# Root-mean-square norms of a transformer kernel: squares, sums and row scale issued at three separate places

## The chip, the cores and the metric

The kernel runs on one core of a Trainium2 chip. Its time is the device time in microseconds (us) of one execution; lower is better. The engines are named as in the profile: PE does the matrix products and PEld loads their stationary operands, DVE is the vector engine, ACT the activation engine, POOL the general one (GpSimd), SP issues the transfers.

## The reference

256 tokens of 1024 features go through two blocks of attention and feed-forward parts, a mixture of experts among them. Every part begins with the same norm, and this norm is what the change is about:

```python
def rms_norm(x, g):
    xf = x.astype(F32)
    y = xf * lax.rsqrt(jnp.mean(xf * xf, axis=-1, keepdims=True) + EPS)
    return (y * g.astype(F32)).astype(x.dtype)
...
    h = rms_norm(x, a_norm_mix[j])
    x = x + diff_attention_mixer(h, mem, ...)
    ...
    x = x + dense_swiglu(rms_norm(x, dense_norm[j]), dense_w_gate_up[j], dense_w_down[j])
```

The gain g is folded into the operand of the products. The factor 1/rms is one number per token and commutes with a product over the features, so the kernel multiplies the unscaled x and scales what comes out.

## The kernel before

The activations x lie with the features on the partitions: four tiles of 128 x 512 (`xpair(i)`, two blocks of 128 features by 256 tokens). Each weight piece of 128 x 1024 is split into a high and a low part, `hi` by ACT (L229) and `lo` by DVE (L230); x is split in the same way into `xh` and `xl`. A product is then three matmuls, xh with hi, xh with lo and xl with hi (L258 to L260 by features, L264 to L266 by tokens). PE does almost nothing else, and it works strictly in the order of its instructions, as do DVE, ACT and POOL. A list scheduler of the framework sets that order when the kernel is built, from the order of the code and its own costs; each instruction waits only for its data and its buffers.

A norm (`stats_r`, 16 of them) goes as follows. ACT squares the four tiles (L334). In the eleven norms of the kind "later", POOL adds them in pairs (L337), so that two tiles of 128 x 512 are left. PE sums over the features: it multiplies each 128 x 128 piece of those tiles with one column of ones (L350, tile `ms`), eight matmuls of 128 x 1, each of which stands in the trace as two records. DVE adds epsilon (L353), POOL takes the power -1/2 (L354): that is `r`, by token on the partitions. Products by features need it along the free dimension: `rows_R` turns it on PE with two transposes (L361, tile `R`), and DVE copies the result out (L365). The eleven are those of layer A, of the memory `mem`, of the dense part, of layer B, of the mixture of experts, and of the start, the feed-forward part and the gate at the end ("ple") of each of the two last blocks. The five others (`final_norm` and the four norms after a part, in `post`) add their squares on DVE (L339) and stand where nothing else is left to multiply.

In the code before, sums and turn stand right behind the squares: `R = stats_R(xpair)`. The scheduler places the first four thin matmuls as soon as it takes the first pair to be ready, the other four when the second pair is, and the transposes a few products behind.

Of the kernel before, what the change touches and what calls it, by code (L numbers as in the profile page):

```python
# [17 lines left out]
EPS = 1e-6  # L18
# [76 lines left out]
# vectors over the features, as columns of 128: (key, how many columns)  # L95
# [15 lines left out]
def layout(v):  # L111
    """the arrays of the launch: the weights as they come, the rest laid out as the chip reads it"""
# [21 lines left out]
def body(ctx: ExitStack, tc: tile.TileContext, I, out, stop=None):  # L134
# [111 lines left out]
    def wpieces(w, k0, kn, c0, width, s):  # L246
        """wtile in pieces of 512, which leaves its tiles to what is under way"""
# [120 lines left out]
    def stats_R(src):  # L368
        return rows_R(stats_r(src))

    def stats(src):
        r = stats_r(src)
        return r, rows_R(r)

# [32 lines left out]
    def feat_1024(X, w, s, order, side=None, hook=None):  # L407
        """X times w, by features; side yields what it makes of X while the rest is multiplied"""
# [67 lines left out]
    def steps(gen, n=None):  # L476
        """runs n steps of a generator (all of them without n); whether it goes on"""
# [10 lines left out]
    def feat_gen(X, w, c0, s, done, loaded=None):  # L488
        wh, wl = wsplit(loaded or wload(w, 0, 8, c0, 256, s))
        ps = PB("fp")  # L490
        for k in range(8):
# [3 lines left out]
            if k == 3:  # L495
                yield 1
        done(ps)
        yield 1

    def tok_gen(X, w, c0, s, done):  # L500
        wh, wl = wtile(w, 0, 8, c0, 256, s)
        ps = PB("tp")
        for k in range(8):
# [3 lines left out]
            if k == 3:  # L507
                yield 1
        done(ps)
        yield 1  # L510

    def feat_pair(X, w, c0, s):
        out = []
        steps(feat_gen(X, w, c0, s, out.append))
        return out[0]
# [4 lines left out]
    def by_R(lst, R, f=None, tile=G):  # L520
        """keeps a product by features, times R"""
        def done(ps):
            g = tile("fT")
            if f is None:
                V.tensor_tensor(r3(g, 2), r3(ps, 2), R2(R), op=OP.mult)
            else:
                V.scalar_tensor_tensor(r3(g, 2), r3(ps, 2), f, R2(R), op0=OP.mult, op1=OP.mult)
# [1310 lines left out]
```

## Time and profile before

| what | value |
|---|---|
| median of 3 runs | 2311.73 us (2307.82 to 2312.98) |
| span of the profiled execution | 2313.2 us |
| instructions | 36939 |
| PE busy | 2239.2 us, 97% of the span |
| DVE busy | 1817.8 us, 79% |
| ACT busy | 1474.7 us, 64% |
| POOL busy | 76.4 us, 3% |
| the thin matmuls of all 16 norms (L350) | 256 records, 35.0 us busy |

The profiled execution is one of its own; its span is 0.06% above the median of the timed runs. Busy times of PE overlap from one matmul to the next, so a busy PE can still be slowed: the granted clock (PEclk) says how fast it could go, 1.00 at the higher of its two levels (2.4 GHz) and 0.50 at the lower (1.2 GHz).

### The profile page before, as it was taken

Reading aid. Unit: us, or ns where it says so; the run is one execution under the profiler, and the core shown is the slowest. Engines: PE = TensorE matmul, PEld = TensorE weight load, DVE = VectorE, ACT = ScalarE, POOL = GpSimd, SP = SyncE. Lnnn points to the kernel's source line nnn. Section 1 sums busy time; section 2 is a strip of 40 time slices with the busy share of each in tenths; the row PEclk is TensorE's granted clock in tenths of the full one; section 3 lists DMA queues with packets and bytes.
Section 4 is the critical chain, followed back from the end, with each engine's and each line's share of the span. In section 5 each row is a group of like instructions: output and inputs, shape, how many; then the busy total and the mean of one; then the engine's idle time right before and its main releaser. Section 6 shows DMA issues by size and latency. Waiting matters only on the chain. (4 is left out here: it accounts for less than half of the span.)

```text
span 2313.2 us, 36939 instructions
## 1 busy us (share of the span) xinstructions
PE 2239.2 (97%) x14218; PEld 2019.2 (87%) x14218; DVE 1817.8 (79%) x2701; ACT 1474.7 (64%) x2138; POOL 76.4 (3%) x83
## 2 busy tenths in 40 slices
PE   8999999998999999999999999999999999989998
PEld 7889999997878888888888888879899998989998
DVE  6666576766888898989898989888777777867776
ACT  5554457435777777777777777777665565765554
POOL 0100001000000000000000000000000001000001
PEclk9999999998999999999999999999999999989998
DMA  8445556224999999999999999986245544525550
GB/s 288 139 137 174 195 171 204 92 78 167 359 348 335 349 353 372 338 354 351 373 350 341 349 378 350 372 299 221 74 136 193 182 147 137 186 78 183 183 178 19
DMA packets 297113, 551.23 MB, mean 238 GB/s; under 512 B 10336, under 2 KB 132064, under 8 KB 296928
## 3 DMA queue, kind: packets, MB, share of 16 engines
q1 hardware_dynamic: 296928, 548.78, 67.5%
q8 instruction: 114, 1.87, 0.3%
q14 instruction: 71, 0.58, 0.1%
HBM read 547.70 MB, written 1.05 MB: 237 GB/s over the span
## 5 line engine op out<-in xcount | busy, mean ns | idle before, releaser
L230 DVE TENSOR_TENSOR loe<-ste,hie 128x1024 fp32r<-128x1024 f32 x448 | 520.0, 1217 | 12.4 <-ACT hie L229 4.2
L229 ACT ACTIVATE hie<-ste 128x1024 fp32r<-128x1024 f32 x448 | 439.5, 1053 | 23.9 <-PE ac L260 9.9
L230 DVE TENSOR_TENSOR lod<-std,hid 128x1024 fp32r<-128x1024 f32 x224 | 264.9, 1218 | 17.1 <-ACT hid L229 15.6
L229 ACT ACTIVATE hid<-std 128x1024 fp32r<-128x1024 f32 x224 | 221.4, 1057 | 4.8 <-PE pg L265 2.3
L266 PE MATMUL pu<-loe,eh 128*128 128x512 f32 x448 | 176.7, 394 | 1.4 <-DVE loe L230 1.4
L1159 PE MATMUL y<-hid,hl 128*128 128x512 f32 x448 | 175.7, 392 | 2.0 <-DVE hl L284 2.0
L264 PE MATMUL pg<-hie,eh 128*128 128x512 f32 x448 | 175.4, 391 | 0.3 <-ACT eh L286 0.3
L266 PE MATMUL pg<-loe,eh 128*128 128x512 f32 x448 | 175.6, 392 | 0.0
L264 PE MATMUL pu<-hie,eh 128*128 128x512 f32 x448 | 174.7, 390 | 0.0
L265 PE MATMUL pg<-hie,el 128*128 128x512 f32 x448 | 174.6, 390 | 0.0
L265 PE MATMUL pu<-hie,el 128*128 128x512 f32 x448 | 174.6, 390 | 0.0
L1158 PE MATMUL y<-hid,hh 128*128 128x512 f32 x448 | 173.4, 392 | 0.7 <-ACT hh L283 0.7
L1137 ACT ACTIVATE eh<-pg,cw 128x512 f32<-128x512 f32 x56 | 38.6, 689 | 203.4 <-PE pg L266 203.4
L1160 PE MATMUL y<-lod,hh 128*128 128x512 f32 x448 | 163.4, 407 | 0.8
L258 PE MATMUL gu<-xh,hig 128*128 128x256 f32 x528 | 150.8, 286 | 3.7 <-ACT xh L286 3.7
L230 DVE TENSOR_TENSOR lou<-stu,hiu 128x1024 fp32r<-128x1024 f32 x66 | 80.4, 1220 | 91.1 <-PE gu L259 82.9
L259 PE MATMUL gu<-xh,log 128*128 128x256 f32 x528 | 150.5, 285 | 0.0
L260 PE MATMUL gu<-xl,hiu 128*128 128x256 f32 x528 | 150.5, 285 | 0.0
L258 PE MATMUL gu<-xh,hiu 128*128 128x256 f32 x528 | 150.4, 285 | 0.0
L259 PE MATMUL gu<-xh,lou 128*128 128x256 f32 x528 | 150.3, 285 | 0.0
L260 PE MATMUL gu<-xl,hig 128*128 128x256 f32 x528 | 150.1, 285 | 0.0
L258 PE MATMUL ac<-hh,hidn 128*128 128x256 f32 x528 | 149.4, 283 | 0.0
(516 smaller groups left out, 6279.5 us busy)
## 6 DMA issues: line engine op xcount, KB each, us to landing
ste<-in_moe_w_gate_up_dram SPq DMA_DIRECT2D x224, 1024.0 KB, 7.2
std<-in_moe_w_down_dram SPq DMA_DIRECT2D x112, 1024.0 KB, 5.5
stg<-in_w_up_dram SPq DMA_DIRECT2D x22, 1024.0 KB, 5.1
stu<-in_w_up_dram SPq DMA_DIRECT2D x22, 1024.0 KB, 5.1
stdn<-in_w_down_dram SPq DMA_DIRECT2D x22, 1024.0 KB, 4.8
stg<-in_dense_w_gate_up_dram SPq DMA_DIRECT2D x11, 1024.0 KB, 5.0
stu<-in_dense_w_gate_up_dram SPq DMA_DIRECT2D x11, 1024.0 KB, 5.0
stdn<-in_dense_w_down_dram SPq DMA_DIRECT2D x11, 1024.0 KB, 4.9
```

The lines of the kernel that those rows point to most:

```text
L229: A.activation(hi[:, :m], sq, AF.Copy)
L230: V.tensor_tensor(lo[:, :m], sq, hi.bitcast(F32)[:, :m], op=OP.subtract)
L258: T.matmul(o, lhsT=lh, rhs=rh, start=start, stop=False, **kw)
L259: T.matmul(o, lhsT=ll, rhs=rh, start=False, stop=False, **kw)
L260: T.matmul(o, lhsT=lh, rhs=rl, start=False, stop=stop, **kw)
L264: T.matmul(o, lhsT=xh, rhs=wh, start=start, stop=False, **kw)
L265: T.matmul(o, lhsT=xl, rhs=wh, start=False, stop=False, **kw)
L266: T.matmul(o, lhsT=xh, rhs=wl, start=False, stop=stop, **kw)
L1137: A.activation(t, pg, AF.Silu, scale=rc)
L1158: T.matmul(y[hf], lhsT=h[:, fs], rhs=a, start=opens, stop=False)
L1159: T.matmul(y[hf], lhsT=l[:, fs], rhs=a, start=False, stop=False)
L1160: T.matmul(y[hf], lhsT=h[:, fs], rhs=b, start=False, stop=ends)
```

## The change

The eleven norms become objects of a class `Norm` with three parts. The squares are made at once; POOL adds only the first two tiles, DVE adds the third and the fourth (L368 of the changed kernel, 128 x 512) and then the halves (L369, 128 x 256), so that 256 columns are left and two thin matmuls do where eight did (four records for sixteen). These are issued when something first asks for `r`, and the transposes when something first asks for `R`. `first_two` asks for r behind the first whole product and for R in the middle of the second; `swiglu_ff` asks for r at step 20 of the 32 of its first pair and for R when that pair is done; `tok_wide` at its second half; the memory's norm does its squares early and its sums at the end of the second group of filling work. The five others (`stats_now`) keep their eight thin matmuls, with the last square made in two halves.

```diff
-    def squares(src, how):
-        """tiles whose sum over features, through the matrix of ones, is the mean square"""
-        sq = [J("sq") for _ in range(4)]
-        for i in range(4):
-            A.activation(sq[i], src(i), AF.Square)
-            if how == "later":
-                if i % 2:
-                    GP.tensor_tensor(sq[i - 1], sq[i - 1], sq[i], op=OP.add)
-            elif i in (1, 2):
-                V.tensor_tensor(sq[0], sq[0], sq[i], op=OP.add)
-        return sq[0:3:2] if how == "later" else sq[0:4:3]
-
-    def stats_r(src, how="later"):
-        """1 / rms over the 1024 features, by token"""
-        tiles = squares(src, how)
+    def mean_square(pieces):
         ps = PC("ms")
-        for n, t in enumerate(tiles):
+        for n, t in enumerate(pieces):
             for c in range(2):
-                for kk in range(2):
-                    o = kk * 256 + c * 128
-                    T.matmul(ps[:, c:c + 1], lhsT=t[:, o:o + 128], rhs=onec, start=n == 0 and c == 0 and kk == 0,
-                             stop=n == len(tiles) - 1 and kk == 1, skip_group_check=True)
+                T.matmul(ps[:, c:c + 1], lhsT=t[:, c * 128:c * 128 + 128], rhs=onec, start=n == 0 and c == 0,
+                         stop=n == len(pieces) - 1, skip_group_check=True)
+        return ps[:, 0:2]
+    def inv_root(ms):
         r, m = S(2, "r"), S(2)
-        V.tensor_scalar(m, ps[:, 0:2], EPS, None, op0=OP.add)
+        V.tensor_scalar(m, ms, EPS, None, op0=OP.add)
         GP.tensor_tensor(r, m, neghalf[:, :2], op=OP.pow)
         return r

+    def stats_now(src):
+        sq = [J("sq") for _ in range(4)]
+        for i in range(3):
+            A.activation(sq[i], src(i), AF.Square)
+            if i:
+                V.tensor_tensor(sq[0], sq[0], sq[i], op=OP.add)
+        for kk in range(2):
+            sl = slice(kk * 256, kk * 256 + 256)
+            A.activation(sq[3][:, sl], src(3)[:, sl], AF.Square)
+        return inv_root(mean_square([t[:, kk * 256:kk * 256 + 256] for t in (sq[0], sq[3]) for kk in range(2)]))
+    class Norm:
+        def __init__(self, src=None):
+            sq = [J("sq") for _ in range(4)]
+            for i in range(4):
+                A.activation(sq[i], (src or xpair)(i), AF.Square)
+                if i == 1:
+                    GP.tensor_tensor(sq[0], sq[0], sq[1], op=OP.add)
+                elif i > 1:
+                    V.tensor_tensor(sq[0], sq[0], sq[i], op=OP.add)
+            V.tensor_tensor(sq[0][:, :256], sq[0][:, :256], sq[0][:, 256:], op=OP.add)
+            self.sq = sq[0][:, :256]
+            self._r = self._R = None
+        @property
+        def r(self):
+            if self._r is None:
+                self._r = inv_root(mean_square([self.sq]))
+            return self._r
+        @property
+        def R(self):
+            if self._R is None:
+                self._R = rows_R(self.r)
+            return self._R
...
-    def tok_wide(X, w, c0, width, s):
+    def tok_wide(X, w, c0, width, s, norm=None):
         pss = [PB("tw"), PB("tw")]
         for kh in range(2):
+            if norm is not None and kh:
+                norm.r
             wh, wl = wtile(w, kh * 4, 4, c0, width, s)
             for k in range(4):
...
-    def feat_gen(X, w, c0, s, done, loaded=None):
+    def feat_gen(X, w, c0, s, done, loaded=None, hold=False):
         wh, wl = wsplit(loaded or wload(w, 0, 8, c0, 256, s))
...
+        if hold:
+            yield 1
         done(ps)
         yield 1
...
+    def first_two(a, b, norm, rows):
+        steps(a, 2)
+        norm.r
+        steps(b, 1)
+        if rows:
+            norm.R
+        steps(a)
+        steps(b)
...
-            for k, b, j in order:
+            for n, (k, b, j) in enumerate(order):
+                if jp == 0 and n == 20:
+                    norm.r
                 wh, wl = ((gh, gl), (uh, ul))[b]
...
-        r, R = stats(xpair)
+        norm = Norm()
...
-        steps(feat_gen(X, w, 0, "q", by_R(qT, R, 0.125), opening))
-        steps(feat_gen(X, w, 768, "k", by_R(kT, R)))
+        first_two(feat_gen(X, w, 0, "q", by_R(qT, norm, 0.125), opening, hold=True),
+                  feat_gen(X, w, 768, "k", by_R(kT, norm)), norm, True)
...
         def mem_stats():
-            shared["rm"] = stats(lambda i: mem[i])
+            shared["rm"] = Norm(lambda i: mem[i])
             yield 1

+        def mem_sums():
+            shared["rm"].r
+            yield 1
         def kv_gen():
-            rm, Rm = shared["rm"]
-            yield from mem_kv(mem, rm, Rm, "a_mem_norm", I["a_w_mem_kv"][0], kv)
+            shared["rm"].R
+            yield from mem_kv(mem, shared["rm"], "a_mem_norm", I["a_w_mem_kv"][0], kv)

         fills = [chain(v_gen(0), qk_gen(1)),
-                 chain(v_gen(1), mem_stats(), qk_gen(2), feat_gen(X, w, 2304, "qm", by_R(qm, R, 0.125))),
+                 chain(v_gen(1), mem_stats(), qk_gen(2), feat_gen(X, w, 2304, "qm", by_R(qm, norm, 0.125)), mem_sums()),
                  chain(v_gen(2), kv_gen())]
         tail = None
         for hp in range(3):
...
+        sums = Norm()
...
-        r = stats_r(xpair)
+        r = sums.r
...
-        for c, ps in enumerate(tok_wide(X, w, 512, 512, "z1")):
+        wide = tok_wide(X, w, 512, 512, "z1", norm)
+        r = norm.r
+        V.tensor_scalar(rq, r, 0.125, None, op0=OP.mult)
+        V.tensor_scalar(rh, r, 0.5, None, op0=OP.mult)
+        for c, ps in enumerate(wide):
...
+        first_two(gate(0), gate(1), norm, True)
+        for n in range(2, 4):
+            steps(gate(n))
```

Three places show how instructions move. Names are tiles, output first, with their numbers; one row of `x4` stands for four matmuls.

PE at the memory's norm in layer A, before; `fp` is a product by features, `ms` the sums, `R` the turn, `at` transposes of attention weights:

```order
L260 MATMUL fp_755<-xl_116,hiq_751 128x256
L350 MATMUL ms_721<-keep,sq_711 128x1 x4
L258 MATMUL fp_755<-xh_115,hiq_751 128x256
...
L259 MATMUL fp_829<-xh_97,lok_822 128x256
L350 MATMUL ms_721<-keep,sq_713 128x1 x4
L260 MATMUL fp_829<-xl_98,hik_821 128x256
...
L260 MATMUL fp_829<-xl_98,hik_821 128x256
L361 MATMUL R_734<-keep,r_730 128x128 x2
L726 MATMUL at_739<-keep,s_571 128x128
```

and in the changed kernel:

```order
L260 MATMUL fp_870<-xl_116,hiqm_866 128x256
L335 MATMUL ms_921<-keep,sq_707 128x1 x2
L737 MATMUL sc_928<-fT_858,fT_790 128x128
...
L293 MATMUL tr_1063<-keep,hn_1001 128x128 x4
L389 MATMUL R_1074<-keep,r_924 128x128 x2
L760 MATMUL at_1138<-keep,s_934 128x128
```

The sums were at two places eleven matmuls apart, and the turn stood four matmuls behind the second; now they stand once, more than a hundred rows later, and the turn some 57 rows behind them.

PE at the gate of the first of the two last blocks, before:

```order
L259 MATMUL fp_32404<-xh_32338,lopg_32397 128x256
L350 MATMUL ms_32376<-keep,sq_32366 128x1 x4
L260 MATMUL fp_32404<-xl_32339,hipg_32396 128x256
...
L258 MATMUL fp_32468<-xh_32348,hipg_32464 128x256
L350 MATMUL ms_32376<-keep,sq_32368 128x1 x4
L259 MATMUL fp_32468<-xh_32348,lopg_32465 128x256
...
L259 MATMUL fp_32468<-xh_32348,lopg_32465 128x256
L361 MATMUL R_32389<-keep,r_32385 128x128 x2
L260 MATMUL fp_32468<-xl_32349,hipg_32464 128x256
```

and in the changed kernel:

```order
L258 MATMUL fp_32429<-xh_32333,hipg_32425 128x256
L335 MATMUL ms_32412<-keep,sq_32341 128x1 x2
L259 MATMUL fp_32429<-xh_32333,lopg_32426 128x256
L260 MATMUL fp_32429<-xl_32334,hipg_32425 128x256
...
L259 MATMUL fp_32429<-xh_32333,lopg_32426 128x256
L260 MATMUL fp_32429<-xl_32334,hipg_32425 128x256
L389 MATMUL R_32454<-keep,r_32415 128x128 x2
L260 MATMUL fp_32503<-xl_32304,hipg_32495 128x256
```

The first four thin matmuls are gone, and the rest is two; between them and the turn stand eleven products where seven stood.

DVE at the router of the mixture of experts, before; `loe` is the low part of an expert's weights, `xl` of the tokens, `lg` the logits, and the reduction of `lg` begins the choice of experts:

```order
L230 TENSOR_TENSOR loe_19564<-ste_19561,hie_19563 128x1024
L424 TENSOR_TENSOR keep<-ac_5532,keep 128x512
L230 TENSOR_TENSOR loe_19568<-ste_19561,hie_19567 128x1024
L284 TENSOR_TENSOR xl_5866<-xt_5870,xh_5862 128x512
L1039 COPY lg_5898<-lg_5845 128x16
L284 TENSOR_TENSOR xl_5868<-xt_5877,xh_5864 128x512
L284 TENSOR_TENSOR xl_5867<-xt_5884,xh_5863 128x512
L284 TENSOR_TENSOR xl_5869<-xt_5891,xh_5865 128x512
L1044 TENSOR_REDUCE s_5900<-lg_5898 128x2
```

and in the changed kernel:

```order
L230 TENSOR_TENSOR loe_19544<-ste_19541,hie_19543 128x1024
L447 TENSOR_TENSOR keep<-ac_5516,keep 128x512
L368 TENSOR_TENSOR sq_5846<-sq_5846,sq_5848 128x512
L284 TENSOR_TENSOR xl_5862<-xt_5866,xh_5858 128x512
L1079 COPY lg_5894<-lg_5829 128x16
L230 TENSOR_TENSOR loe_19548<-ste_19541,hie_19547 128x1024
L368 TENSOR_TENSOR sq_5846<-sq_5846,sq_5849 128x512
L284 TENSOR_TENSOR xl_5864<-xt_5873,xh_5860 128x512
L369 TENSOR_TENSOR sq_5846<-sq_5846 128x256
L284 TENSOR_TENSOR xl_5863<-xt_5880,xh_5859 128x512
L284 TENSOR_TENSOR xl_5865<-xt_5887,xh_5861 128x512
L1084 TENSOR_REDUCE s_5896<-lg_5894 128x2
```

Three additions of squares are new ahead of that reduction, and the second `loe` has moved from ahead of the copy of the logits to behind it.

## Rows read from the trace of the kernel before

**Rows 1.** The page, busy time and share of the span by engine.

```profile
PE 2239.2 (97%) x14218; PEld 2019.2 (87%) x14218; DVE 1817.8 (79%) x2701; ACT 1474.7 (64%) x2138; POOL 76.4 (3%) x83
```

**Rows 2.** Groups by line: busy us, mean ns | idle us before, releaser.

```profile
L337 POOL TENSOR_TENSOR sq<-sq,sq 128x512 f32<-128x512 f32 x22 | 36.1, 1643 | 327.9 <-ACT sq L334 291.0 <-PE ac L260 13.6 <-issue 10.7
...
L350 PE MATMUL ms<-keep,sq 128*128 128x1 f32 x256 | 35.0, 259 | 7.5 <-POOL sq L337 4.4 <-DVE sq L339 2.6 <-ACT sq L334 0.2
...
L354 POOL TENSOR_TENSOR r<-s,keep 128x2 f32<-128x2 f32 x16 | 18.5, 1154 | 1464.8 <-DVE s L353 1460.2 <-DVE s L1069 4.6
...
L361 PE MATMUL R<-keep,r 128*128 128x128 f32 x26 | 6.4, 334 | 8.5 <-POOL r L354 8.4
```

**Rows 3.** DVE adds of squares: duration ns min/median/max.

```profile
L339 DVE TENSOR_TENSOR sq<-sq,sq x10: 680/691/694, 1541.4 to 2269.2; 128x512 f32<-128x512 f32 x10
```

**Rows 4.** Timeline, layer A: start us, us, engine, line.

```profile
13.51 1.08 PE L350 MATMUL ms<-keep,sq 128*128 128x1 f32 x8
...
14.90 2.13 DVE L230 TENSOR_TENSOR loq<-stq,hiq 128x1024 fp32r<-128x1024 f32 x1 [3.86 <-PE fp L259]
...
17.09 0.53 PE L259 MATMUL fp<-xh,loq 128*128 128x256 f32 x1 [2.04 <-DVE loq L230]
...
18.05 1.70 PE L350 MATMUL ms<-keep,sq 128*128 128x1 f32 x8
```

**Rows 5.** Timeline of PE, the norm of mem.

```profile
67.46 1.06 PE L350 MATMUL ms<-keep,sq 128*128 128x1 f32 x8 [0.99 <-POOL sq L337]
...
70.88 1.70 PE L350 MATMUL ms<-keep,sq 128*128 128x1 f32 x8
...
74.53 0.69 PE L361 MATMUL R<-keep,r 128*128 128x128 f32 x2 [0.89 <-POOL r L354]
```

**Rows 6.** Stretches: us, busy PE PEld DVE ACT POOL, PEclk, DMA share, GB/s.

```profile
13.50:20.00 6.50, 4.46 (x26) 4.25 (x26) 3.13 (x5) 5.19 (x8) 1.28 (x1) 0.78 0.73 224
20.00:26.00 6.00, 6.00 (x37) 6.00 (x37) 5.33 (x6) 1.06 (x1) 1.64 (x1) 0.67 0.74 249
66.40:78.00 11.60, 9.72 (x49) 9.35 (x48) 5.59 (x8) 3.61 (x5) 3.85 (x3) 0.59 0.43 152
148.00:157.00 9.00, 7.06 (x58) 6.86 (x59) 6.29 (x10) 4.03 (x8) 3.88 (x3) 1.00 0.12 34
```

**Rows 7.** Timeline of PE, the norms of the dense part and of layer B.

```profile
148.68 1.05 PE L350 MATMUL ms<-keep,sq 128*128 128x1 f32 x8 [0.79 <-POOL sq L337]
...
152.32 0.95 PE L350 MATMUL ms<-keep,sq 128*128 128x1 f32 x8
...
155.22 0.43 PE L361 MATMUL R<-keep,r 128*128 128x128 f32 x2 [1.26 <-POOL r L354]
...
353.12 1.84 PE L350 MATMUL ms<-keep,sq 128*128 128x1 f32 x16
...
357.57 0.43 PE L361 MATMUL R<-keep,r 128*128 128x128 f32 x2 [1.07 <-POOL r L354]
```

**Rows 8.** Timeline, ple gate of block 0, start of block 1.

```profile
1911.31 0.47 PE L361 MATMUL R<-keep,r 128*128 128x128 f32 x2 [1.03 <-POOL r L354]
...
1930.35 1.75 DVE L1748 TENSOR_TENSOR keep<-keep,sg 128x512 f32<-128x512 f32 x1
...
1931.61 1.49 PE L350 MATMUL ms<-keep,sq 128*128 128x1 f32 x8 [1.76 <-POOL sq L337]
1932.14 0.91 ACT L286 ACTIVATE xh<-keep 128x256 fp32r<-128x256 f32 x2 [1.59 <-DVE keep L1748]
```

**Rows 9.** Timeline of DVE, router of the mixture of experts.

```profile
518.20 1.21 DVE L230 TENSOR_TENSOR loe<-ste,hie 128x1024 fp32r<-128x1024 f32 x1
...
523.24 0.17 DVE L1039 COPY lg<-lg 128x16 f32<-128x16 f32 x1 [1.41 <-PE lg L1016]
...
525.85 0.16 DVE L1044 TENSOR_REDUCE s<-lg 128x2 f32<-128x16 f32 x1
...
538.83 0.69 DVE L1089 TENSOR_TENSOR oh<-mc,keep 128x512 fp32r<-128x512 f32 x1 [6.57 <-DVEq L1202]
```

More of the change, by code (lines that the diff above doesn't have):

```diff
@@ L366, in rows_R @@
         return R[:, :256]
[L368 to L373, printed above, removed]
     def R2(R):
@@ L508, in tok_gen, with by_R @@
                 yield 1
+        if hold:
+            yield 1
         done(ps)
         yield 1
[L512 to L515, printed above, removed]
+    def first_two(a, b, norm, rows):
[6 more added lines that the diff above has]
+        steps(b)
     def GK(s):
         return gp.tile([128, 512], F32, tag="kv", name=nm(s), bufs=N_KV)
-    def by_R(lst, R, f=None, tile=G):
+    def by_R(lst, norm, f=None, tile=G):
         def done(ps):
@@ L611, in head_rms, with swiglu_ff @@
         yield 1
-    def swiglu_ff(X, R, w_gu, w_d, dff, conv=None, hook=None):
+    def swiglu_ff(X, norm, w_gu, w_d, dff, conv=None, hook=None):
         nj = dff // 128
@@ L639, in swiglu_ff @@
                 jj = jp * 2 + j
-                V.tensor_tensor(r3(t, 2), r3(ps, 2), R2(R), op=OP.mult)
+                V.tensor_tensor(r3(t, 2), r3(ps, 2), R2(norm.R), op=OP.mult)
                 y = t
@@ L811, in gates @@
             f, k = G("f"), G("k")
-            hp = len(fs)
+            hp, r = len(fs), norm.r
+            if hp == 0:
+                V.tensor_scalar(rn, r, -1.0, None, op0=OP.mult)
             for c in range(2):
@@ L823, in silu @@
         def silu(ps):
-            sg = G("sg")
+            sg, r = G("sg"), norm.r
             for c in range(2):
@@ L829, in silu @@
             sgs.append(sg)
-        for hp in range(3):
-            steps(tok_gen(X, w, 768 + hp * 256, "fz", gates))
+        first_two(tok_gen(X, w, 768, "fz", gates, hold=True), tok_gen(X, w, 1024, "fz", gates), norm, False)
+        steps(tok_gen(X, w, 1280, "fz", gates))
         for hp in range(3):
@@ L838, in layer_b @@
         for hp in range(3):
-            steps(feat_gen(X, w, hp * 256, "q", by_R(qT, R)))
+            steps(feat_gen(X, w, hp * 256, "q", by_R(qT, norm)))
             f = fs[hp]
@@ L964, in i_gen @@
         def i_gen(hp):
[L965 removed]
+            return tok_gen(X, w, 1536 + hp * 256, "i", by_r(vts, norm))
         def ma_gen():
             yield from mem_attn(qm[0], kv_b[0], kv_b[1], XC)
[L970 removed]
+        fill = chain(i_gen(0), i_gen(1), feat_gen(X, w, 3072, "qm", by_R(qm, norm, 0.125)), ma_gen(), i_gen(2))
         outs = iter(())
@@ L1206, in final_norm @@
     def final_norm(fill, cols):
-        r = stats_r(xpair, "now")
+        r = stats_now(xpair)
         fill(0)
@@ L1740, in second, with gate, done @@
             return
-        R = stats_R(xpair)
-        for n in range(4):
-            ps = feat_pair(X, I["w_ple_gate_2"][i], n * 256, "pg")
-            t = G2("sg")
-            V.tensor_tensor(r3(t, 2), r3(ps, 2), R2(R), op=OP.mult)
-            A.activation(t, t, AF.Tanh, scale=0.5)
-            V.scalar_tensor_tensor(t, t, 1.0, pj[n], op0=OP.add, op1=OP.mult)
-            V.tensor_tensor(xpair(n), xpair(n), t, op=OP.add)
-            if i == 1 and stop is None:
-                nc.sync.dma_start(out[:, 2 * n:2 * n + 2, :], xr[:, 2 * n:2 * n + 2, :])
+        norm = Norm()
+        def gate(n):
+            def done(ps):
+                t = G2("sg")
+                V.tensor_tensor(r3(t, 2), r3(ps, 2), R2(norm.R), op=OP.mult)
+                A.activation(t, t, AF.Tanh, scale=0.5)
+                V.scalar_tensor_tensor(t, t, 1.0, pj[n], op0=OP.add, op1=OP.mult)
+                V.tensor_tensor(xpair(n), xpair(n), t, op=OP.add)
+                if i == 1 and stop is None:
+                    nc.sync.dma_start(out[:, 2 * n:2 * n + 2, :], xr[:, 2 * n:2 * n + 2, :])
+            return feat_gen(X, I["w_ple_gate_2"][i], n * 256, "pg", done, hold=n == 0)
+        first_two(gate(0), gate(1), norm, True)
+        for n in range(2, 4):
+            steps(gate(n))
         return prep(colf("pre_mix_g_21")) if i == 0 else None
@@ L1774, in run @@
                 return
-            R = stats_R(xpair)
-            acc = swiglu_ff(X, R, I["dense_w_gate_up"][0], I["dense_w_down"][0], 2816, hook=lower_bounds)
+            norm = Norm()
+            acc = swiglu_ff(X, norm, I["dense_w_gate_up"][0], I["dense_w_down"][0], 2816, hook=lower_bounds)
             kv_b = []
-            steps(mem_kv(mem, *shared["rm"], "b_mem_norm", I["b_w_mem_kv"][0], kv_b))
+            steps(mem_kv(mem, shared["rm"], "b_mem_norm", I["b_w_mem_kv"][0], kv_b))
             X = add_prep(acc, colf("b_norm_mix"))
```

41 lines of the change are left out of this document (18 added, 23 removed).

## The prediction

> **What bounds the kernel now.** The page comes first: PE is busy 97% of the span, DVE 79%, ACT less, POOL 3% [rows 1]. A change pays if it takes instructions, waits or half-clock time from PE, and costs if it makes PE wait longer for DVE. The groups by line then say what the norms take there. The 256 records of thin matmuls (L350) are busy 35.0 us and PE stood idle 7.5 us in front of them, 4.4 of it for POOL's additions; the 26 transposes (L361) had 8.4 us of idle time for POOL's power [rows 2]. The timelines of the eleven places say which of this lies on the path, and the stretches show the granted clock around them.
>
> One record costs more than nothing although it multiplies one column. In layer B 16 of them take 1.84 us [rows 7]; without the last one's 0.26 [rows 2] that is 15 steps of 0.105 us. At the lower clock, 8 take 1.70 us at the memory's norm [rows 5], steps of 0.21.
>
> **What it removes.** Each of eleven norms goes from 16 records to 4, 132 fewer in all. The 12 of the mixture of experts are not on the path (DVE's choice of experts ends later than they do), so 120 count: 120 x 0.105 = 12.6 us. Two groups of 8 ran at the lower clock (layer A's second, the memory's second [rows 4, 5]), 0.1 more for each record, 1.6. Together **14.2**. The four that stay are in this sum.
>
> The Trainium skill (TensorE: Matmul & The Clock Gate, "Wait — 56ns, not 53.3ns?") puts the least start-to-start time of small matmuls at about 25 ns. By that, the removed records would be worth 120 x 0.025 = 3.0 us instead of 14.2, and the whole sum below would be 11.8. The trace shows four times that step, and I go by the trace; that floor stays as a rival.
>
> **Waits for the squares.** Of the 4.4 us, 0.99 stand at the memory [rows 5], 0.79 at the dense part [rows 7] and 1.76 at the start of block 1 [rows 8]. Now the sums come half a product or more behind the squares, so POOL's first addition and DVE's two have several us of products over them. I count them gone but for the 1.76: there the next product needs the operand xh, which ACT starts only at 1932.14, half a us after the thin matmuls begin [rows 8]. That place stays late, now waiting for xh. Gain 4.4 - 1.76 = **2.6**. If only half of the cover holds it is 1.3.
>
> **Waits for the turn.** In the dense part the second group ends at 152.32 + 0.95 = 153.27 and the transposes start at 155.22 [rows 7]: the chain of epsilon, power and hand-overs takes 1.95 us. Behind the memory, the dense part and layer B the turn now has 36 or more products over it, or is not asked for until much later; 0.89, 1.26 and 1.07 go [rows 5, 7], 3.2 together. At the feed-forward parts and gates of the last two blocks only eleven products lie between sums and turn. A product takes 0.12 (58 records, busy 7.06 [rows 6]), so 1.3 of 1.95 are covered and 0.6 are left, against 1.03 before at the first gate [rows 8]: 0.4 gained at one such place. For the four I take 0.8 in all and not 1.6, because at two of them DVE's epsilon stands behind a low part of weights (1.21 [rows 9]) that waits for PE itself. Bounds: 0 if that low part always delays it, 3 if the power takes well under its mean of 1.154 [rows 2], so that the eleven products cover the chain. Gain **4.0**.
>
> **Layer A's wait.** PE waits 2.04 us for loq, and that split took 2.13 us while POOL added squares [rows 4]; the same kind takes 1.21 elsewhere [rows 9]. The second POOL addition is gone and the first is early. What is late next is still loq, because it waits for a product of PE, but 0.9 shorter: **0.9**, between 0 and 2.
>
> **The clock.** The rows show that the clock fell where waits and thin matmuls came together, and stayed at 1.00 in the dense part in spite of waits of 0.79 and 1.26 [rows 6, 7]. In 66.40 to 78.00 its mean is 0.59, that is 82% or 9.5 us at the lower level; without the wait of 0.89 and 1.7 us of thin matmuls, both counted above, 6.9 us of other work ran at half speed, a loss of 3.4. Layer A's two stretches, 0.78 of 6.5 and 0.67 of 6.0 us, give 2.9 + 4.0 = 6.8, without 1.7 of thin matmuls 5.1, a loss of 2.6 [rows 6]. Around the memory's norm nothing but whole products is left, so I take 2.5 of the 3.4. In layer A a wait of about 1.1 remains, and I take 1.0 of 2.6. At the start of block 1 the wait remains and so, I think, does the fall; nothing is counted. Gain **3.5**, between 0 and 6.0.
>
> **What it adds.** DVE gets 22 additions at 0.69 us [rows 3] and 11 of half the size, which the trace does not show; half of 0.69 and a little, 0.41, makes 15.2 + 4.5 = 20 us. POOL loses eleven additions of 1.64 [rows 2]. Where does DVE stand on the path? Within long products it has idle time enough, as PE waits for it hardly at all: those are costed at nothing, and their cover is DVE's free fifth; 1.8 us per norm if that cover is gone. In the mixture of experts there is no cover. The choice of experts starts at 525.85, 2.61 after the copy of the logits at 523.24, and the experts can't begin before it is through: the branch holds everything until 538.83 [rows 9]. Now 1.21 of loe (which stood in idle time ahead of it), one addition of 0.69 and the half of 0.41 come between, 2.3 in all. Of this 0.5 disappears in waits for xh that those three splits had before: **+1.8**, between 1.5 and 2.3. The four norms of `post` make the last square in two halves; the sums of its first half can go earlier, but two instructions take longer than one. Half a tenth to three tenths each, **+0.4**.
>
> **Sum.** -14.2 - 2.6 - 4.0 - 0.9 - 3.5 + 1.8 + 0.4 = -23.0 us against the profiled execution's span of 2313.2, 2290.2. That execution is 1.5 above the median of the timed runs, 2311.7, and from this the forecast is **2288.7**.
>
> **Rivals.** (1) *The idle time moves.* PE always waits for whatever is late; with the sums gone from their place it waits at the same product for a low part, for xl or for transposes' operands. What speaks for it is the start of block 1, where xh is only 0.5 behind [rows 8], and layer A. Against it: in the dense part and layer B nothing but the norm itself ends a wait [rows 7]. Then the waits (7.5) and the clock (3.5) are not gained: -14.2 + 2.2 = -12, 2299.7. (2) *A thin record is worth a quarter of its step*, 0.025, since what it really blocks is short: -23.0 + 14.2 - 3.0 = -11.8, 2299.9. The 0.105 of layer B speaks against it. That is the floor of the Trainium skill named above. (3) *No change.* DVE's 20 us come to lie on the path wherever a norm stands, since a norm stands just where operands are being made. 11 x 1.8 = 20 against 23 leaves -3, 2308.5. For it: 79% busy. Against it: PE's waits at the norms are for POOL, not for DVE splits, save one in layer A [rows 2, 4]. (4) *Slower.* DVE's first addition must wait for POOL's, which takes 1.64 in the mean [rows 2], and the splits that make the next operands stand behind it in DVE's order. All eleven norms have this order. A wait of 1.64 and 1.8 of work would be 3.4 each, 38 in all, net +15: 2327. It decides from 2.1 us for each norm (23 / 11). Against it: DVE stood idle 3.86 us at the norm of layer A [rows 4], and ACT makes the squares one behind the other, so POOL's addition runs while the third square is made.
>
> **How the numbers follow.** The forecast's case has 0.67, (1) 0.19, (2) 0.02, (3) 0.07, (4) 0.05. Its own range follows from the bounds: with the whole clock (6.0), the turn's 3 instead of 0.8 and layer A's 2.0 it is -28.8, 2282.9; with none of the clock, half of the squares' wait, nothing for loq, no gain at the four last turns and +2.3, it is -16.0, 2295.7. The range takes in rival (1) and a part of what lies between it and (3): 2280 to 2304. A measurement of this kernel can tell about 0.2%, 4.6 us, from no change. Faster by more than that: the forecast, (1) and (2), 0.88; within it (3), 0.07; slower (4), 0.05.
>
> **What would show it.** Thin matmuls: 5 x 16 + 11 x 4 = 124 records, some 17 us busy. No PE idle time at the sums for POOL. At the memory's norm a granted clock of 1.00 through the same products; in layer A a wait for loq of about 1.1. Turns: waits of 0.6 or so at the four places of the last blocks and none at the other norms. The choice of experts 4.4 us behind the copy of the logits instead of 2.6. The prediction is wrong if PE waits for DVE's additions or for splits behind them (rivals 3 and 4), or if the lower clock is found again over the same products with another wait ahead of it (rival 1).

## The result and the profile after

The changed kernel takes 2280.84 us (median of 4 runs, 2277.86 to 2282.96) against 2311.89 (4 runs, 2307.82 to 2312.98): a ratio of 0.987, 95% interval 0.9857 to 0.9882, 31 us less. The forecast was 2288.7 in a range of 2280 to 2304. Direction and range held, at the range's lower edge; the gain was 31 where 23 was forecast. The bounds that the prediction adds up itself end at 2282.9; only the widening to 2280, for which it gives no reason, takes the measured time in. The profiled execution of the changed kernel has a span of 2277.9 us and took 2279.79.

The page's busy times after, by engine, answer to [rows 1]:

```profile
PE 2207.9 (97%) x14086; PEld 1989.3 (87%) x14086; DVE 1828.6 (80%) x2734; ACT 1475.4 (65%) x2143; POOL 57.9 (3%) x72
```

PE's share is what it was, but it has 132 records fewer; DVE has 33 instructions more. PE is busy for 31.3 us less; its idle time, the span less the busy time, went only from 74.0 to 70.0. The groups by line (busy us, mean ns | idle us before, releaser) answer to [rows 2]; L366 and L368 are the additions on POOL and DVE, L335 the sums (L351 are DVE's additions in the five other norms), L389 the turn, which waits for POOL's power (L342):

```profile
L366 POOL TENSOR_TENSOR sq<-sq,sq 128x512 f32<-128x512 f32 x11 | 18.0, 1633 | 283.4 <-ACT sq L364 265.0 <-DVE xl L287 18.3
...
L368 DVE TENSOR_TENSOR sq<-sq,sq 128x512 f32<-128x512 f32 x22 | 15.0, 683 | 2.6 <-POOL sq L366 2.6
...
L335 PE MATMUL ms<-keep,sq 128*128 128x1 f32 x124 | 16.9, 251 | 5.6 <-DVE sq L351 2.7 <-DVE sq L369 2.7
...
L389 PE MATMUL R<-keep,r 128*128 128x128 f32 x26 | 5.5, 295 | 5.0 <-POOL r L342 5.0
```

The sums are 124 records, 16.9 us busy, as forecast. No sum waits for POOL any more, but 2.7 us are waited for DVE's last addition (L369), 1.65 of them at the router, off the path, and DVE itself stood 2.6 us for POOL. The turn's waits went from 8.4 to 5.0.

The timeline of layer A (start us, us, engine, line) answers to [rows 4]:

```profile
13.94 1.23 DVE L230 TENSOR_TENSOR loq<-stq,hiq 128x1024 fp32r<-128x1024 f32 x1 [0.84 <-PE fp L259]
...
15.22 0.38 PE L259 MATMUL fp<-xh,loq 128*128 128x256 f32 x1 [1.05 <-DVE loq L230]
...
18.20 0.50 PE L335 MATMUL ms<-keep,sq 128*128 128x1 f32 x4
...
22.14 0.43 PE L389 MATMUL R<-keep,r 128*128 128x128 f32 x2 [0.59 <-POOL r L342]
```

The wait for loq is 1.05 where 2.04 stood, and loq takes 1.23 instead of 2.13. The sums stand once, and the turn waits 0.59, which was not there before. At the memory's norm, the answer to [rows 5], nothing waits:

```profile
77.07 0.50 PE L335 MATMUL ms<-keep,sq 128*128 128x1 f32 x4
...
86.83 0.38 PE L389 MATMUL R<-keep,r 128*128 128x128 f32 x2
```

The stretches (us, busy PE PEld DVE ACT POOL, PEclk, DMA share, GB/s) answer to [rows 6]; the third is the memory's squares and the products that followed them, the last the start of block 1:

```profile
13.50:20.00 6.50, 5.45 (x44) 5.25 (x44) 6.06 (x9) 5.03 (x8) 0.68 (x1) 1.00 0.97 319
20.00:26.00 6.00, 5.41 (x46) 5.21 (x46) 4.91 (x11) 3.60 (x5) 2.08 (x1) 1.00 1.01 331
62.00:75.00 13.00, 12.28 (x103) 12.07 (x102) 8.92 (x13) 6.01 (x8) 0.86 (x1) 1.00 0.57 181
1905.00:1918.00 13.00, 11.96 (x57) 9.45 (x56) 10.35 (x20) 7.17 (x11) 3.58 (x10) 1.00 0.47 140
```

All four have a granted clock of 1.00. In [rows 6] it was 0.78 and 0.67 in layer A and 0.59 at the memory. The timeline of the first gate, the start of block 1 and one of the later turns answers to [rows 8]:

```profile
1890.83 0.39 PE L389 MATMUL R<-keep,r 128*128 128x128 f32 x2
...
1907.51 0.69 DVE L368 TENSOR_TENSOR sq<-sq,sq 128x512 f32<-128x512 f32 x1 [1.18 <-POOL sq L366]
...
1908.84 0.91 ACT L286 ACTIVATE xh<-keep 128x256 fp32r<-128x256 f32 x2 [2.21 <-DVE keep L1791]
...
1912.86 0.61 PE L335 MATMUL ms<-keep,sq 128*128 128x1 f32 x4 [1.04 <-DVE sq L369]
...
2058.70 0.43 PE L389 MATMUL R<-keep,r 128*128 128x128 f32 x2 [0.54 <-POOL r L342]
```

The first gate's turn waits for nothing. At the start of block 1 the sums still wait 1.04 us, for DVE's addition, which stood 1.18 for POOL's; xh is made some 3 us ahead of that and holds up nobody. The router on DVE answers to [rows 9]; L1129 is the first work behind the branch:

```profile
504.05 0.17 DVE L1079 COPY lg<-lg 128x16 f32<-128x16 f32 x1 [0.96 <-PE lg L1055]
...
508.01 0.16 DVE L1084 TENSOR_REDUCE s<-lg 128x2 f32<-128x16 f32 x1
...
514.28 0.15 DVE L1125 CAST cnt_i<-s 128x1 int32<-128x1 f32 x1
519.62 0.69 DVE L1129 TENSOR_TENSOR oh<-mc,keep 128x512 fp32r<-128x512 f32 x1 [5.19 <-SPq L1242]
```

From the copy of the logits to the start of the choice it takes 3.96 us instead of 2.61. From the start of the choice to the count (`cnt_i`) it takes 6.27, as good as in the kernel before (6.26). Behind the count, the branch takes 5.19 where it took 6.57 [rows 9].

### The profile page after: what moved, and what is told of

The parts are those of the page before. It is cut to its first block, busy times and chain, and to the rows that moved or that the text cites. A ratio compares the mean times of both kernels' runs of the same rounds, so it can differ in the third digit from the quotient of the medians.

```text
span 2277.9 us, 36689 instructions
## 1 busy us (share of the span) xinstructions
PE 2207.9 (97%) x14086; PEld 1989.3 (87%) x14086; DVE 1828.6 (80%) x2734; ACT 1475.4 (65%) x2143; POOL 57.9 (3%) x72
## 3 DMA queue, kind: packets, MB, share of 16 engines
HBM read 547.70 MB, written 1.05 MB: 241 GB/s over the span
## 4 chain that ended last, share of the span: by engine, by line
PE 67%; DVE 5%; ACT 2%; issue 2%; POOL 1%; DMA 0%; POOLq 0%; DVEq 0%; ACTq 0%; SPq 0%
PE y L1200 5%; PE pg L266 4%; PE y L1199 4%; PE y L1198 4%; PE pg L264 4%; PE pg L265 4%; PE pu L266 4%; PE pu L264 4%; PE pu L265 4%; PE gu L260 4%; PE gu L258 4%; PE gu L259 4%; PE ac L259 2%; PE ac L258 2%; PE ac L260 2%
## 5 line engine op out<-in xcount | busy, mean ns | idle before, releaser
L230 DVE TENSOR_TENSOR lod<-std,hid 128x1024 fp32r<-128x1024 f32 x224 | 265.0, 1220 | 17.1 <-ACT hid L229 15.6
L230 DVE TENSOR_TENSOR lou<-stu,hiu 128x1024 fp32r<-128x1024 f32 x66 | 80.5, 1221 | 88.6 <-PE gu L259 77.2
```

Source lines behind the costliest of these rows:

```text
L230: V.tensor_tensor(lo[:, :m], sq, hi.bitcast(F32)[:, :m], op=OP.subtract)
```

## The experiments

Nine variants were run, and both kernels once more. Where two are compared that ran beside different runs of the kernel before, their ratios say the same as the differences of the medians unless the text gives both. A profile's idle time of PE is its span less PE's busy time on the page; in the changed kernel's two profiles it is 70.0 us.

**Six more thin matmuls: what does a thin record cost?**

```diff
+        for n in range(extra):
+            for c in range(2):
+                o = 2 + 2 * n + c
+                T.matmul(ps[:, o:o + 1], lhsT=pieces[0][:, c * 128:c * 128 + 128], rhs=onec, start=False, stop=True,
+                         skip_group_check=True)
...
```

(`extra` is 3.)

> The changed kernel with six more thin matmuls at each of the eleven norms, whose results nobody reads: the 132 records are back, behind one another and without any other work of POOL or DVE. At 0.105 us for each of the 120 on the path 2293.5 us; at 0.025 for each 2284 us. If thin records themselves bring the lower clock, it is found again behind them and the time is above 2296 us.

Measured: 2295.37 us (2294.22 to 2296.58), ratio 0.9922 (0.9906 to 0.9939): 14.5 us more than the changed kernel by the medians, 12 by the ratios. The timeline of PE in the dense part and at the start of block 1, where L340 are the added records:

```profile
144.71 0.50 PE L335 MATMUL ms<-keep,sq 128*128 128x1 f32 x4
145.07 1.48 PE L340 MATMUL ms<-keep,sq 128*128 128x1 f32 x12
...
1921.79 0.61 PE L335 MATMUL ms<-keep,sq 128*128 128x1 f32 x4 [1.04 <-DVE sq L374]
1922.26 1.95 PE L340 MATMUL ms<-keep,sq 128*128 128x1 f32 x12
```

In the dense part 12 added records take 1.48 us, steps of (1.48 - 0.26) / 11 = 0.11; the ten norms on the path make 10 x 12 x 0.11 = 13 us. The total holds more than the records: PE is busy for 2229.7 us, 20 to 22 more than in the two profiles of the changed kernel, and its idle time is 65.1, 5 less, since the records also fill waits. The floor of 0.025 of rival (2) is refuted. The Trainium skill (TensorE: Matmul & The Clock Gate, "LDWEIGHTS (loading the stationary operand)") gives a weight load as its columns divided by 1.2, in ns: 107 for 128 columns. This agrees with the 0.11 of the row, at a granted clock of 1.00; at the lower level the steps were 0.21 [rows 5], and the figure of the Trainium skill does not tell the two apart. The trace has 132 loads of 128 x 128 for the 132 added records. But each product of 128 x 256 brings such a load too and takes 0.12 [rows 6], and no run has a thin matmul without a load; that the load is the cause is argued from the equal size. The stretches of the same kernel show a second thing:

```profile
143.00:152.00 9.00, 9.00 (x79) 9.00 (x78) 5.59 (x8) 3.47 (x4) 1.62 (x1) 1.00 0.68 223
1919.00:1931.00 12.00, 10.96 (x44) 8.68 (x43) 6.13 (x14) 4.42 (x6) 0.80 (x2) 0.72 0.30 85
```

16 thin records in a dense stream left the clock at 1.00 in the dense part; the same 16 behind a wait of 1.04 at the start of block 1 are followed by 0.72, where the four of the changed kernel, behind the same wait, are followed by 1.00.

**Two thin matmuls, but early**

```diff
             self._r = self._R = None
+            self.r
+            if rows:
+                self.R
...
-        steps(a, 2)
-        norm.r
-        steps(b, 1)
-        if rows:
-            norm.R
         steps(a)
         steps(b)
...
```

(At the router, not shown here, the squares too are made later, behind the choice of experts.)

> The two thin matmuls and the DVE additions stay, but sums and turn are issued right behind the squares again and the first two products of a part one after the other. In the order of PE this moves them at layer A, the memory, the dense part, layer B and the router; at the last two blocks they stand where the changed kernel has them. If the count of thin records and the dense stream that follows from it made the gain, only waits for the turn come back, 0.6 us at each of four places: 2283 us (2281 to 2287), and the granted clock stays at 1.00 through layer A and the memory. If the late place made it, the waits and the lower clock of layer A and the memory come back, 3 + 3.4 + 4.7 us: 2292 us.

Measured: 2285.94 us (2285.59 to 2286.31), ratio 0.9884 (0.9867 to 0.99): 5.1 more than the changed kernel by the medians, 3 by the ratios. The memory's sums and their stretch:

```profile
66.66 0.60 PE L335 MATMUL ms<-keep,sq 128*128 128x1 f32 x4 [0.57 <-DVE sq L369]
```

```profile
62.00:75.00 13.00, 12.37 (x102) 11.76 (x101) 8.66 (x14) 5.52 (x7) 1.57 (x2) 1.00 0.50 165
```

The sums wait 0.57 for DVE here, in the same place where eight of them waited 0.99 for POOL [rows 5], and the clock stays at 1.00. PE is busy for 2208.0 us, as in the changed kernel; its idle time is 75.6, some 5.5 more. So the early place costs 3 to 5 us, in waits alone, with two thin matmuls, nearer to the first view (up to 2287) than to the second (2292).

**Eight thin matmuls, but late**

```diff
-                if i == 1:
-                    GP.tensor_tensor(sq[0], sq[0], sq[1], op=OP.add)
-                elif i > 1:
-                    V.tensor_tensor(sq[0], sq[0], sq[i], op=OP.add)
-            V.tensor_tensor(sq[0][:, :256], sq[0][:, :256], sq[0][:, 256:], op=OP.add)
-            self.sq = sq[0][:, :256]
+                if i % 2:
+                    GP.tensor_tensor(sq[i - 1], sq[i - 1], sq[i], op=OP.add)
+            self.sq = [t[:, kk * 256:kk * 256 + 256] for t in (sq[0], sq[2]) for kk in range(2)]
...
```

> The late places stay, but POOL adds in pairs and each of the eleven norms has eight thin matmuls again, as before; DVE adds nothing. If a thin record costs 0.105 us wherever it stands, 120 of them on the path cost 12.6: 2293 us, and up to 2299 with layer A's wait and clock, since the scheduler puts its sums early again. If place is what counts and thin records hide, 2282 to 2284 us.

Measured: 2296.03 us (2293.68 to 2297.16), ratio 0.9923 (0.9906 to 0.9941): 15.2 more than the changed kernel by the medians, 12 by the ratios. Layer A's sums, which the scheduler put early all the same, and the memory's, which stand late; then the sums at the start of block 1 and the stretches of all three:

```profile
14.13 0.95 PE L335 MATMUL ms<-keep,sq 128*128 128x1 f32 x8
...
16.69 1.25 PE L335 MATMUL ms<-keep,sq 128*128 128x1 f32 x8 [0.40 <-POOL sq L366]
...
79.95 1.84 PE L335 MATMUL ms<-keep,sq 128*128 128x1 f32 x16
...
1922.08 1.05 PE L335 MATMUL ms<-keep,sq 128*128 128x1 f32 x8 [1.31 <-POOL sq L366]
```

```profile
14.00:20.00 6.00, 5.36 (x34) 4.95 (x33) 5.06 (x6) 4.61 (x7) 3.57 (x2) 0.78 0.97 314
76.00:92.00 16.00, 15.59 (x128) 14.15 (x127) 10.21 (x33) 7.45 (x18) 1.72 (x2) 1.00 0.41 133
1919.00:1931.00 12.00, 10.63 (x53) 8.32 (x53) 7.56 (x14) 5.71 (x9) 3.19 (x9) 1.00 0.34 99
```

At the memory 16 records stand together behind no wait, and the clock is 1.00. In layer A it is 0.78. At the start of block 1 eight records follow a wait of 1.31, and there too it is 1.00: a wait with thin matmuls behind it does not always bring the fall.

With the kernel before, four kernels can be set side by side: eight and early 2311.9, eight and late 2296.0, two and early 2285.9, two and late 2280.8. They make no clean square: early means the first five places, since behind the experts all but the kernel before have their code late; and with eight, the scheduler put not only layer A's sums early but also those of the first gate in two groups 6.3 us apart (1888.68 and 1894.97), as before. So the 16 us between the first two hold eleven places, and the 5 us between the last two hold five; from the first to the third both the count and six of the places change. What can be read is that two instead of eight gains 15 us with late code, and that the gains don't add. In PE's idle time the late place shows by itself: 74.0 and 77.2 us in two profiles of the kernel before, 65.1 here.

**The memory's norm alone as before**

```diff
-            shared["rm"] = Norm(lambda i: mem[i])
+            shared["rm"] = Norm(lambda i: mem[i], pairs=True)
...
```

(With `pairs`, POOL adds in pairs, eight thin matmuls follow, and r and R are asked for at once.)

> The changed kernel with the memory's norm alone as before: added in pairs by POOL, eight thin matmuls and the turn at the old rows of PE's order. If wait and thin matmuls together bring the lower clock there, the whole step of that place comes back, 7 us: 2288 us, with the clock below 1.00 behind the memory's sums. If the fall needs what came before it in layer A or comes by chance, only 1.3 us of thin matmuls and 1.9 of waits come back: 2284 us.

Measured: 2285.15 us (2284.23 to 2287.78), ratio 0.989 (0.987 to 0.9911), 4.3 more than the changed kernel. The memory's rows and their stretch:

```profile
62.76 1.05 PE L335 MATMUL ms<-keep,sq 128*128 128x1 f32 x8 [0.99 <-POOL sq L366]
...
65.80 1.70 PE L335 MATMUL ms<-keep,sq 128*128 128x1 f32 x8
...
69.45 0.69 PE L394 MATMUL R<-keep,r 128*128 128x128 f32 x2 [0.89 <-POOL r L342]
```

```profile
62.00:74.00 12.00, 10.35 (x53) 10.06 (x54) 5.29 (x8) 3.62 (x5) 3.54 (x3) 0.59 0.49 170
```

The rows of before are back, to the hundredth in their waits, and with them the clock of 0.59, without any fall in layer A ahead of it. So the place makes the fall: the second view's reason is refuted. Its number, 2284, is nearer than the first view's 2288; the profiled execution, span 2283.7, is 5.8 above the changed kernel's. Without the 3.2 of thin matmuls and waits, 1.1 by the medians and 2.6 by the profiles are left for the clock at this place.

**Both kernels once more**

> The kernel before once more, one look: whether the lower clock at layer A, the memory, the first gate and the start of block 1 is found again at the same work (if the work sets it, it is, some 13 us lost there), and whether the branch before the experts takes 6.6 us again or the 4.9 to 5.3 of the other kernels.

> The changed kernel once more, to see what of its profile repeats. If the lower clock falls at places that the work sets, layer A and the memory stay at 1.00 and the gates of the last blocks show no fall of their own, and about 28 us of the profile are lost to it in all; if the falls come by chance, they stand elsewhere this time. Time 2281 us.

Measured: the kernel before 2306.85 us in one run, 5 below the median of the runs beside it; the changed kernel 2280.33 (2277.86 to 2281.89), ratio 0.987 (0.985 to 0.989). Stretches of the kernel before in its second profile: layer A, the memory, the first gate, the start of block 1:

```profile
13.00:20.00 7.00, 4.77 (x38) 4.17 (x37) 5.40 (x6) 5.42 (x8) 3.57 (x2) 1.00 0.98 316
64.00:75.00 11.00, 9.85 (x60) 9.56 (x61) 4.80 (x8) 3.62 (x5) 3.06 (x3) 0.69 0.50 163
1904.00:1912.00 8.00, 6.97 (x59) 6.77 (x59) 6.02 (x9) 3.60 (x4) 1.69 (x2) 1.00 0.43 136
1926.00:1936.00 10.00, 9.98 (x45) 8.46 (x46) 4.24 (x8) 3.60 (x5) 2.08 (x3) 0.83 0.45 145
```

The fall at the memory and at the start of block 1 are there again, but milder; those of layer A and of the first gate are not. So the expectation held for two places of four. In the changed kernel's second profile all four are at 1.00, as in its first.

Layer A differs in more than the clock. In the first profile of the kernel before, POOL's second addition began ahead of the split of loq; in the second one behind it:

```profile
14.68 1.28 POOL L337 TENSOR_TENSOR sq<-sq,sq 128x512 f32<-128x512 f32 x1 [2.27 <-ACT sq L334]
```

```profile
14.13 1.22 DVE L230 TENSOR_TENSOR loq<-stq,hiq 128x1024 fp32r<-128x1024 f32 x1 [2.96 <-ACT xh L286]
...
14.56 1.94 POOL L337 TENSOR_TENSOR sq<-sq,sq 128x512 f32<-128x512 f32 x1 [2.20 <-ACT sq L334]
...
15.41 0.39 PE L259 MATMUL fp<-xh,loq 128*128 128x256 f32 x1 [1.14 <-DVE loq L230]
```

Each time the one that began second took longer: the split 2.13 beside POOL's 1.28 [rows 4], and POOL 1.94 beside the split's 1.22. With the split first, PE waits 1.14 for loq and not 2.04, as long as in the changed kernel's second profile.

The pages of the two second profiles, first of the kernel before, then of the changed one:

```profile
PE 2227.9 (97%) x14218; PEld 2007.7 (87%) x14218; DVE 1818.3 (79%) x2701; ACT 1474.2 (64%) x2138; POOL 76.8 (3%) x83
```

```profile
PE 2209.3 (97%) x14086; PEld 1991.3 (87%) x14086; DVE 1828.8 (80%) x2734; ACT 1475.0 (65%) x2143; POOL 57.5 (3%) x72
```

Their spans are 2305.1 and 2279.3 us. The mean granted clock over the span is 0.977 and 0.982 in the two profiles of the kernel before, 0.985 and 0.983 in those of the changed one. Time at the lower level is (1 - clock) x span / 0.5: 106 and 83 us before, 68 and 78 after. One execution differs from another of the same program by more than the term that I had forecast. The branch took 6.48 us in the kernel before's second profile, 4.8 to 5.3 in all ten profiles of kernels with the change beside the first.

**All additions on DVE**

```diff
-                    GP.tensor_tensor(sq[0], sq[0], sq[1], op=OP.add)
+                    V.tensor_tensor(sq[0], sq[0], sq[1], op=OP.add)
```

> The changed kernel with the first addition of squares on DVE too: 11 more additions of 0.69 us there, and POOL adds nothing. If DVE's additions lie beside other work and its wait for POOL (2.6 us in all) cost something, the time is 2279 to 2281 us. If DVE's additions are on the path, 11 x 0.69 = 7.6 us come on top: 2288 us.

Measured: 2273.56 us (2270.88 to 2277.02), ratio 0.9839 (0.9819 to 0.9859), beside the changed kernel's 2280.33 on the same chip. This beats both. Its groups by line:

```profile
L368 DVE TENSOR_TENSOR sq<-sq,sq 128x512 f32<-128x512 f32 x22 | 15.1, 685 | 0.1
...
L335 PE MATMUL ms<-keep,sq 128*128 128x1 f32 x124 | 17.3, 255 | 4.4 <-DVE sq L351 2.7 <-DVE sq L369 1.7
...
L389 PE MATMUL R<-keep,r 128*128 128x128 f32 x26 | 5.6, 297 | 3.5 <-POOL r L342 3.5
```

DVE's wait for POOL is gone (0.1 for 2.6), the sums wait 1.7 for DVE's additions instead of 2.7 (what is left stands at the router, off the path), and the turn 3.5 instead of 5.0. These two waits of PE make 2.5 us. In the profiles PE's idle time is 64.9 us (2275.0 - 2210.1), 5 less than the changed kernel's: the other 2.5 are waits of 1.1 for DVE's `rep` and of 0.7 each for ACT's `aT` and `u`, which are gone too. Why these go was not tested, and of the 6.8 between the medians some 2 stay open.

**DVE's additions twice**

```diff
+            V.tensor_tensor(sq[2], sq[2], sq[3], op=OP.add)
+            V.tensor_tensor(sq[2], sq[2], sq[3], op=OP.add)
+            V.tensor_tensor(sq[2][:, :256], sq[2][:, :256], sq[3][:, :256], op=OP.add)
```

> The changed kernel with the three DVE operations of each norm issued a second time on tiles that nobody reads: 33 more, 1.8 us for each norm. If DVE has cover everywhere but at the router, the router's 1.4 to 2 us come on top, 2283 us. If DVE stands on the path at the norms, 11 x 1.8 = 20 us come on top: 2300 us, and half of it 2291 us.

Measured: 2283.28 us (2281.41 to 2284.91), ratio 0.9888 (0.9868 to 0.9907): 3.0 more than the changed kernel on the same chip, as the first view has it. 20 us of additions cost 3, and 1.3 of these lie at the router, where the way from the logits' copy to the count takes 11.55 us (507.18 to 518.73) where the changed kernel takes 10.23 (504.05 to 514.28). At the other norms DVE has cover for nearly all of them.

**The router's norm in pairs on POOL, the last square whole**

> The changed kernel with the last square of the five other norms made whole again. I expected 0.4 us of cost from the halves, so 2280.4 us; the other view is that the halves let sums start earlier and save something, 2282 us. Both lie near what can be told from no change.

```diff
-        for kk in range(2):
-            sl = slice(kk * 256, kk * 256 + 256)
-            A.activation(sq[3][:, sl], src(3)[:, sl], AF.Square)
+        A.activation(sq[3], src(3), AF.Square)
```

Measured with the whole square alone: 2279.31 us (2278.44 to 2281.14), ratio 0.9857 (0.9841 to 0.9874). That is 1.5 less than the changed kernel by the medians, 3 by the ratios, with intervals that overlap: it can't be told from the changed kernel.

> The changed kernel with the router's norm alone added in pairs by POOL and summed in eight thin matmuls, and the last square of the five other norms whole. From the copy of the logits to the count of the experts' tokens the changed kernel takes 10.2 us, the one before 8.9: if DVE's additions are what lies between, it is 8.9 again and the time 2279.5 us. If something else holds the choice of experts, it stays at 10.2 and 2281 us.

```diff
-        sums = Norm()
+        sums = Norm(pairs=True)
...
```

Measured: 2279.34 us (2276.46 to 2281.58), ratio 0.9871 (0.9853 to 0.989). DVE at the router:

```profile
503.87 0.17 DVE L1080 COPY lg<-lg 128x16 f32<-128x16 f32 x1 [0.66 <-PE lg L1056]
...
506.48 0.16 DVE L1085 TENSOR_REDUCE s<-lg 128x2 f32<-128x16 f32 x1
...
512.74 0.15 DVE L1126 CAST cnt_i<-s 128x1 int32<-128x1 f32 x1
```

The choice starts 2.61 us behind the copy of the logits as in [rows 9], and the count is 8.9 behind it. So DVE's additions and the moved split are what costs 1.35 us there (1.0 against the second profile of the kernel before, where the choice starts 3.0 behind the copy); in the time it can't be told from no change (1.0 less than the changed kernel beside it).

> All additions of squares on DVE but those of the router's norm, which POOL makes in pairs with eight thin matmuls, and the last square of the five other norms whole. If the two edits add up, the router's 1.35 us come off the time of the kernel with all additions on DVE: 2272 us. If that kernel's time was luck, 2279 us.

Measured: 2276.23 us (2274.21 to 2277.05), ratio 0.9849 (0.9832 to 0.9866). All nine runs of the two kernels with these additions on DVE lie below all eight runs of the changed kernel (2277.05 at most, 2277.86 at least), so that moving them gains something. That the two edits add up is not shown: the median lies above that of the single edit.

## Why the prediction was right, and where its sizes were off

**Thin records, -14.2.** Right: 0.11 each in a dense stream, 12 to 14.5 us by the kernel with six more; by PE's busy times (below) some 16 for all 132 records, with the 12 off the path.

**Waits for the squares, -2.6.** Here a step failed: "That place stays late, now waiting for xh." The order of PE before shows what stood behind the first sums at the start of block 1:

```
L266 MATMUL tw_32703<-loz_8380_32712,xh_32656 128x512
L350 MATMUL ms_32686<-keep,sq_32676 128x1 x4
L264 MATMUL tw_32704<-hiz_8379_32711,xh_32656 128x512
```

The product behind the sums uses the same xh as the one ahead of them, so it was ready; only the sums held PE. The xh of 1932.14 in [rows 8] belonged to later products. The changed kernel has xh 3 us ahead there. Of 1.76 us, 1.04 were still waited, for DVE's addition and not for xh; with all additions on DVE no wait is left. Gain 4.4 - 1.04 = 3.4.

**Waits for the turn, -4.0.** 8.4 - 5.0 = 3.4. The 1.95 of the chain against eleven products' 1.3 gave 0.6, and 0.54 was measured at the last blocks' second feed-forward part and second gate; at the first feed-forward part it was 1.15, where none stood before, behind the low part of weights that the prediction named, and at the first gate nothing.

**Layer A's wait, -0.9.** 2.04 - 1.05 = 1.0 in the first profiles, and nothing between the second ones (1.14 and 1.14). The long split was that of an execution in which POOL began first; that the term fits the first pair is luck. What the prediction didn't name is the turn's 0.59 there.

**The clock, -3.5.** The mechanism was right; the size depends on the execution. Sums that stand early and in pairs brought the lower clock at the memory in all three profiles that have them, and in none of the ten that have them late or only two of them. In the first pair of profiles the whole of the memory's and layer A's loss went, not a part, and that of the start of block 1 went too, which I had counted at nothing for the reason above. PE's busy time gives the size, because the products are the same before and after. Added up from the traces, PE was busy at the lower level for 85.3 and 61.1 us before, 50.5 and 55.2 after. A product there takes 0.21 us for 0.12 (128 x 256) or 0.43 for 0.23 (128 x 512), so some 0.45 of this time is lost to the clock; that is an estimate. Without the loss, the busy time is 2200.8 and 2200.4 before, 2185.2 and 2184.5 after: the same in two executions of one program, as it should be, and the difference is the thin records.

| us less | first profiles | second profiles |
|---|---|---|
| thin records (PE busy) | 15.6 | 15.9 |
| clock (PE busy) | 15.7 | 2.7 |
| PE idle | 4.0 | 7.2 |
| span | 35.3 | 25.8 |

The timed runs lie between. 16 of the 23 runs of the kernel before beside the experiments have a mean granted clock of 0.977 to 0.980 (spans of 2308.9 to 2316.5), the other seven 0.981 to 0.983 (2304.5 to 2306.6). At 0.982 and 0.983, five of these have a mean span of 2305.5 and five runs of the changed kernel one of 2279.3: 26 us at the same clock. That leaves some 5 of the median's 31 to the clock, an estimate, inside the prediction's bounds of 0 to 6. A part of my error was to size terms from one execution whose clock was lower than that of the next one.

**The waits together.** The waits named above, with the router's and the branch's change, make 3.4 + 3.4 + 1.0 - 1.35 + 1.4 = 7.9 us in the first pair; PE's idle time fell by 4.0 only. So rival (1) was right in part: PE now waits for work that it did not wait for before, 1.6 for DVE's `rep` in block 0, 0.7 each for ACT's `aT` and `u`, 0.5 and 0.4 for `xl`, 3.9 together (other waits rose and fell by as much as each other). Its price was not right: it had no gain left from waits or clock.

**DVE's additions, +1.8, and the halves, +0.4.** 1.0 to 1.35 at the router, shown by the norm in pairs there, and nothing that can be told for the halves. By the page DVE's busy time rose by 10.8 us and not by the 20 of the prediction. Rival (4) had its mechanism, DVE waiting for POOL with splits behind it, but not its price: 2.6 us of waits in all and some 7 by the kernel without POOL's additions, not 38. Rival (3) fell with the doubled additions.

**Not foreseen:** the branch before the experts takes 1.2 to 1.8 us less in every kernel with the change. Its cause stays open: no experiment was made on it.

## What to carry to other kernels

A matmul of one column cost nearly what one of 256 columns did (0.11 and 0.12 us), so fold the data on a vector engine that has idle time before PE sums it, and check this by putting the removed instructions back as dead work. An in-order engine loses time where a short wait sits in front of work that is ready: put the waiting instruction behind that work, and read from the order, not from a neighbouring row, what really stands next. The clock's falls and the order in which two engines begin can differ from one execution to the next; read two profiles of the same program before sizing a term by one of them, and split the change of the span into PE's busy and idle time.

## What the runs showed of the hardware

The granted clock behind the same rows of the same program differs from one execution to the next: layer A's 0.78 was 1.00 in the second profile, the memory's 0.59 was 0.69. At the start of block 1 it fell behind a wait of 1.04 us with 16 thin records (0.72), but not behind the same wait with 4, nor behind 1.31 with eight. Of a DVE split of 128 x 1024 and a POOL addition of 128 x 512 that overlapped at the same place, the one that began second took longer: the split 2.13 for 1.22, or the addition 1.94 for 1.28. The same branch took 6.57 and 6.48 us in one program and 4.8 to 5.3 in the changed kernel and its variants.
